# Reciprocal roots of eight and twelve columns: Newton steps on VectorE in place of powers on GpSimd

## The chip, the cores and the metric

The kernel runs on one core of one Trainium2 chip. The metric is the device time of one execution in microseconds, the median of several runs. TensorE (PE), VectorE (DVE), ScalarE (ACT), GpSimd (POOL) and SyncE (SP, which here only issues DMAs) run side by side and wait for each other by semaphores.

## What is computed

A two-layer backbone for 512 latent and 256 context tokens of width 1024. The first layer joins a gated DeltaNet (its inputs go through a convolution of five taps) with multi-head latent attention, the second a neighbourhood attention with grouped-query attention; a SwiGLU network follows each. The parts that the change touches are norms over the 64 channels of a head:

```python
def rms_norm(x, g):                       # queries and keys of grouped-query attention, layer two
    xf = x.astype(jnp.float32)
    y = xf * lax.rsqrt(jnp.mean(xf * xf, -1, keepdims=True) + NORM_EPS)
    return (y * g.astype(jnp.float32)).astype(x.dtype)

def l2_normalize(x):                      # queries and keys of the DeltaNet, layer one
    xf = x.astype(jnp.float32)
    return (xf * lax.rsqrt(jnp.sum(xf * xf, -1, keepdims=True) + NORM_EPS)).astype(x.dtype)
...
    qkv = jax.nn.silu(short_conv(qkv, conv_w))
    q, k, v = jnp.split(qkv, [GDN_QK_W, 2 * GDN_QK_W], axis=-1)
    q = l2_normalize(q.reshape(b, t_len, GDN_HEADS, GDN_DK)) * (GDN_DK ** -0.5)
    k = l2_normalize(k.reshape(b, t_len, GDN_HEADS, GDN_DK))
```

## The kernel before

Tokens are tiled by 128. Matmuls run in three products of a high and a low half (`mm3`, L198 to L200; in `tok_proj` L548 to L550), so every weight is split on arrival: `split` copies the high half on ScalarE (L181) and subtracts on VectorE (L182). The order of the instructions on each engine is not the order of the program: `TileContext(nc, schedule_with_timeline_sim=True)` plans it, from the order of the program as priority and from its own estimate of what each instruction takes; a few `issue_after` blocks and manual dependencies pin single places.

Convolution stage, layer one. A loop takes twelve blocks of 128 channels, in the order 4 to 7, 0 to 3, 8 to 11. For each, `chan_proj` multiplies the block out on TensorE (tile `qkv`), and the first half of `conv_tail` copies it (L702, L703), convolves it with five VectorE instructions (tile `cy`, L705 and L707) and puts a silu over it (tile `cz`, L709). The second half of `conv_tail` belongs to the block before: TensorE transposes it back into two PSUM banks `pa` and `pb` (L714), ScalarE squares it (L723), VectorE sums the squares over 64 channels to twelve columns, six tiles of tokens by two heads (L726), `rsqrt_` makes the reciprocal root, and VectorE multiplies the two banks by it (L730). Blocks 0 to 7, queries and keys, take this way, so there are eight calls; blocks 8 to 11 are only copied. The product goes to DRAM and, for the keys (4 to 7), through four more GpSimd products (`ek`, `kd`, L741). GpSimd also makes the tiles `gi` (L674) in the first part of the stage, and scales the small projection of the latent attention (L768, L769). The banks `pa` and `pb` come from the tag `v`, which has two banks; the transposes of `mla_latent` (tile `smT`, L775) take a bank of the same tag. The gate projection (`gate_evac`, L842 to L844) runs in the middle of the loop.

Head norms, layer two. `head_norm` runs for four tiles of latent queries (eight columns), `keys_norm` for the keys (eight and four columns). Each squares on ScalarE (L1897, L1920), sums on VectorE (L1900, L1923), takes the root, multiplies on VectorE (L1902, L1925), multiplies by the gain on GpSimd (L1903, L1926) and rotates, on VectorE and GpSimd (`rope`, L394 to L399). Squares and the rotation's products share one buffer, tag `hsq`. In the same stretch the modulation of the second layer is summed on VectorE: `Mod.step` loads a row block (`mraw`) through SP into one of two buffers and adds it with L255. All loads of weights go through the same SP queue, in order.

`rsqrt_` is two GpSimd instructions: an add (L222) and a power with a tile of -0.5 (L229). It has seven call sites; three of them are changed: L728, L1901 and L1924. The others (norms of one or two columns, and L1305 in `gdn_out`, eight columns) stay.

Of the kernel before, what the change touches and what calls it, by code (L numbers as in the profile page):

```python
# [150 lines left out]
F32 = mybir.dt.float32  # L151
F32R = mybir.dt.float32r
F16 = mybir.dt.float16
I32 = mybir.dt.int32
AF = mybir.ActivationFunctionType
ALU = mybir.AluOpType
AX = mybir.AxisListType
PSUM = bass.MemoryType.PSUM
EPS = 1e-6
# [4 lines left out]
def emit(tc, A):  # L164
    nc = tc.nc
    V, S, G, T = nc.vector, nc.scalar, nc.gpsimd, nc.tensor
    es = ExitStack()

    def pool(name, stack, bufs=1, **kw):
        return stack.enter_context(tc.tile_pool(name=name, bufs=bufs, reuse_waits="tile", **kw))  # L170
# [4 lines left out]
    def bc(ap, n):  # L175

        return ap.unsqueeze(len(ap.shape)).to_broadcast(list(ap.shape) + [n])
# [26 lines left out]
    sm = pool("sm", es, bufs=4)  # L204
# [15 lines left out]
    def rsqrt_(out, ss, add):  # L220

        G.tensor_scalar(out, ss, add, None, ALU.add)  # L222
        n = 1
        for s in out.shape[1:]:
            n *= s
        nh = nhalf[:, :n]
        if len(out.shape) == 3:
            nh = nh.rearrange("p (a b) -> p a b", a=out.shape[1])
        G.tensor_tensor(out, out, nh, ALU.pow)  # L229


    cs = cp.tile([128, 8, 2], F32, name="cs", tag="cs")
# [466 lines left out]
    def conv_tail(i, pl, pc):  # L699
# [4 lines left out]
        y = cvp.tile([128, 772], F32, tag="cy", name="cy", bufs=2)  # L704
# [12 lines left out]
        if i >= 8:  # L717
            for ps, a, b in views:
                S.activation(dst[:, a:b, :], ps[:, :(b - a) * 128].rearrange("p (t c) -> p t c", c=128), AF.Copy)
        else:  # L720
            sq = cvp.tile([128, 12, 64], F32, tag="sq", name="sq")
            for ps, a, b in views:
                S.activation(sq[:, 2 * a:2 * b, :], ps[:, :(b - a) * 128].rearrange("p (t c) -> p t c", c=64), AF.Square,  # L723
                             scale=8.0 if i < 4 else 1.0)
            ss = sm.tile([128, 12], F32, tag="ss12", name="ss12")
            V.tensor_reduce(ss, sq, AX.X, ALU.add)  # L726
            r = sm.tile([128, 12], F32, tag="r12", name="r12")
            rsqrt_(r, ss, (64.0 if i < 4 else 1.0) * EPS)  # L728
            for ps, a, b in views:
                V.tensor_tensor(dst[:, a:b, :].rearrange("p t (h c) -> p t h c", h=2),  # L730
                                ps[:, :(b - a) * 128].rearrange("p (t h c) -> p t h c", h=2, c=64),
                                bc(r[:, 2 * a:2 * b].rearrange("p (t h) -> p t h", h=2), 64), ALU.mult)
# [312 lines left out]
    def r3(ap):  # L1045
        return ap.rearrange("p (h c) -> p h c", c=64)
# [846 lines left out]
    def head_norm(dst, ps, nh, gain, t, scale):  # L1893

        sq = bx.tile([128, 512], F32, tag="hsq", name="hsq")
        S.activation(dst, ps, AF.Copy)
        S.activation(sq[:, :nh * 64], dst, AF.Square, scale=scale)  # L1897
        ss = sm.tile([128, 8], F32, tag="oss", name="oss")
        r = sm.tile([128, 8], F32, tag="orr", name="orr")
        V.tensor_reduce(ss[:, :nh], r3(sq[:, :nh * 64]), AX.X, ALU.add)  # L1900
        rsqrt_(r[:, :nh], ss[:, :nh], scale * scale * 64.0 * EPS)  # L1901
        V.tensor_tensor(r3(dst), r3(dst), bc(r[:, :nh], 64), ALU.mult)  # L1902
        G.tensor_tensor(r3(dst), r3(dst), gain.unsqueeze(1).to_broadcast([128, nh, 64]), ALU.mult)  # L1903
        if t < 4:
            rope(bx.tile([128, 512], F32, tag="hsq", name="rp"), r3(dst), ropeg[:, t, 0:32], ropeg[:, t, 32:64], 32, nh)
# [9 lines left out]
    def keys_norm(a, b):  # L1915

        n = 2 * (b - a)
        x = gkt[:, a:b, :].rearrange("p t c -> p (t c)")
        sq = bx.tile([128, 512], F32, tag="hsq", name="hsq")
        S.activation(sq[:, :n * 64], x, AF.Square, scale=0.125)  # L1920
        ss = sm.tile([128, 8], F32, tag="oss", name="oss")
        r = sm.tile([128, 8], F32, tag="orr", name="orr")
        V.tensor_reduce(ss[:, :n], r3(sq[:, :n * 64]), AX.X, ALU.add)  # L1923
        rsqrt_(r[:, :n], ss[:, :n], EPS)  # L1924
        V.tensor_tensor(r3(x), r3(x), bc(r[:, :n], 64), ALU.mult)  # L1925
        G.tensor_tensor(r3(x), r3(x), gkn.unsqueeze(1).to_broadcast([128, n, 64]), ALU.mult)  # L1926
        if a:
            return
        x1, x2 = [gkt[:, 0:4, :].rearrange("p t (h c) -> p t h c", h=2)[:, :, :, i:i + 32] for i in (0, 32)]
        cb, sb = [ropeg[:, 0:4, i:i + 32].unsqueeze(2).to_broadcast([128, 4, 2, 32]) for i in (0, 32)]  # L1930
        tmp = bx.tile([128, 512], F32, tag="hsq", name="rp")
        ta, tb = [tmp[:, i:i + 256].rearrange("p (t h c) -> p t h c", t=4, h=2) for i in (0, 256)]
        V.tensor_tensor(ta, x2, sb, ALU.mult)
        V.tensor_tensor(tb, x1, sb, ALU.mult)
        G.tensor_tensor(x1, x1, cb, ALU.mult)
        G.tensor_tensor(x2, x2, cb, ALU.mult)
        G.tensor_tensor(x1, x1, ta, ALU.subtract)
        G.tensor_tensor(x2, x2, tb, ALU.add)
# [394 lines left out]
```

## Time and profile before

| | |
|---|---|
| time, median of 3 runs | 1955.46 us (1953.3 to 1959.17) |
| the profiled execution's own time | 1962.06 us |
| its span, on which all times of the trace are counted | 1960.3 us |
| mean granted TensorE clock of the span | 0.964 |
| busy: PE, DVE, ACT, POOL | 1825.0, 1411.3, 986.4, 765.9 us |

A row of a group gives line, engine, operation, what it writes and reads, and the count. "Idle before" is how long the engine stood still just ahead of these instructions, and what released it. [...] The names of tiles leave out numbers, so the roots of twelve and of two columns are both `r`.

### The profile page before, as it was taken

The numbers are of one execution on the slowest core, as the hardware profiler recorded it, in microseconds if no ns is written. First come the engines' busy times: TensorE is split into PE (matmuls) and PEld (weight loads), VectorE is DVE, ScalarE is ACT, GpSimd is POOL, SyncE is SP. The second block draws the span as 40 slices with busy tenths as digits, with TensorE's granted clock in tenths as the row PEclk, the third lists the DMA queues.
The fourth block names the chain that finished last, engine by engine and source line by source line (L and its number), as shares of the span: only waits on it lengthen the run. The fifth ranks groups of instructions, "written<-read, shape, count | busy, mean of one in ns | idle before, by whom it ended". The sixth has DMA issues, their size and how long they took to land.

```text
span 1960.3 us, 33838 instructions
## 1 busy us (share of the span) xinstructions
PE 1825.0 (93%) x12780; PEld 1504.9 (77%) x12780; DVE 1411.3 (72%) x2166; ACT 986.4 (50%) x1880; POOL 765.9 (39%) x702
## 2 busy tenths in 40 slices
PE   6989978988998989999999999989999979999998
PEld 4877854655665879999998777877655669999886
DVE  3687767677875596666567897886566589999654
ACT  4433466766874473333334346723355465455443
POOL 2287455354515246566561011253356123333002
PEclk8999988998998999999999999999999979999999
DMA  8255595556643633222227553685443213233221
GB/s 308 88 147 148 187 291 167 178 184 171 211 113 117 232 108 104 96 65 74 78 65 262 162 177 106 215 287 192 153 118 113 87 65 106 91 109 95 88 96 65
DMA packets 125751, 280.20 MB, mean 143 GB/s; under 512 B 12882, under 2 KB 43498, under 8 KB 125588
## 3 DMA queue, kind: packets, MB, share of 16 engines
q1 hardware_dynamic: 125588, 278.03, 44.9%
q8 instruction: 101, 1.65, 0.4%
q14 instruction: 62, 0.51, 0.1%
HBM read 226.15 MB, written 46.07 MB: 139 GB/s over the span
## 4 chain that ended last, share of the span: by engine, by line
PE 62%; DMA 5%; ACT 5%; DVE 4%; issue 2%; POOL 2%; SPq 0%; POOLq 0%; DVEq 0%; ACTq 0%
PE st L199 10%; PE st L200 10%; PE st L198 10%; PE dn L1719 5%; PE dn L1720 5%; PE dn L1721 5%; PE po L189 2%; DMA mraw<-in_wmb_dram 2%; PE y L1435 1%; PE y L1436 1%; PE y L1437 1%; PE st L1981 1%; PE st L1982 1%; PE naqk L198 1%; PE nav L548 1%
## 5 line engine op out<-in xcount | busy, mean ns | idle before, releaser
L198 PE MATMUL st<-ub,hi_gu 128*128 128x384 f32 (+1 forms) x1232 | 385.5, 314 | 8.4 <-ACT ub L181 8.4
L199 PE MATMUL st<-ub,hi_gu 128*128 128x384 f32 (+1 forms) x1232 | 384.3, 312 | 3.0 <-DVE ub L182 3.0
L200 PE MATMUL st<-ub,lo_gu 128*128 128x384 f32 (+1 forms) x1232 | 385.6, 313 | 0.0
L198 PEld LDWEIGHTS st<-ub,hi_gu 128*128 128x128 f32 x1232 | 234.2, 190 | 8.8 <-ACT ub L181 8.8
L199 PEld LDWEIGHTS st<-ub,hi_gu 128*128 128x128 f32 x1232 | 234.8, 191 | 3.7 <-DVE ub L182 3.6
L200 PEld LDWEIGHTS st<-ub,lo_gu 128*128 128x128 f32 x1232 | 233.4, 189 | 0.5
L181 ACT ACTIVATE hi_gu<-s 128x512 fp32r<-128x512 f32 x176 | 110.9, 631 | 173.6 <-PE st L199 161.0
L1719 PE MATMUL dn<-hi_wd,gh 128*128 128x512 f32 x440 | 174.5, 397 | 2.2 <-ACT gh L181 2.2
L1720 PE MATMUL dn<-lo_wd,gh 128*128 128x512 f32 x440 | 174.0, 396 | 0.0
L1721 PE MATMUL dn<-hi_wd,gl 128*128 128x512 f32 x440 | 162.7, 400 | 1.6 <-DVE gl L182 1.6
L182 DVE TENSOR_TENSOR lo_gu<-s,hi_gu 128x512 fp32r<-128x512 f32 x154 | 129.1, 839 | 44.3 <-ACT hi_gu L181 44.2
L182 DVE TENSOR_TENSOR lo_gu<-raw_gu,hi_gu 128x512 fp32r<-128x512 f32 x132 | 130.0, 998 | 41.2 <-ACT hi_gu L181 41.1
L181 ACT ACTIVATE hi_gu<-raw_gu 128x512 fp32r<-128x512 f32 x132 | 81.9, 629 | 98.5 <-PE st L199 92.8
L255 DVE SCALAR_TENSOR_TENSOR macc<-mraw,cs,macc 128x1024 f32<-128x1024 f32 x80 | 104.5, 1322 | 17.9 <-DMA mraw<-in_wmb_dram 13.9
L1629 POOL TENSOR_TENSOR s<-raw_gu 128x512 f32<-128x512 f32 x44 | 75.4, 1713 | 99.8 <-issue 62.6
L929 ACT ACTIVATE P<-st 128x512 f32<-128x512 f32 x128 | 73.0, 596 | 73.4 <-PE st L200 36.0
L1719 PEld LDWEIGHTS dn<-hi_wd,gh 128*128 128x128 f32 x440 | 82.7, 188 | 23.3 <-ACT gh L181 2.7
L181 ACT ACTIVATE gh<-g 128x512 fp32r<-128x512 f32 x76 | 47.7, 631 | 104.7 <-PE dn L1720 95.2
L1721 PEld LDWEIGHTS dn<-hi_wd,gl 128*128 128x128 f32 x440 | 82.0, 188 | 23.5 <-DVE gl L182 3.5
L182 DVE TENSOR_TENSOR gl<-g,gh 128x512 fp32r<-128x512 f32 x76 | 54.3, 719 | 61.8 <-ACT gh L181 56.3
L1720 PEld LDWEIGHTS dn<-lo_wd,gh 128*128 128x128 f32 x440 | 82.7, 188 | 20.4 <-issue 0.7
L1685 POOL TENSOR_TENSOR g<-g,up 128x512 f32<-128x512 f32 x38 | 55.7, 1466 | 89.0 <-DVE up L1634 57.5
(540 smaller groups left out, 4702.3 us busy)
## 6 DMA issues: line engine op xcount, KB each, us to landing
mraw<-in_wmb_dram SPq DMA_DIRECT2D x56, 512.0 KB
raw_wd<-in_wd_dram SPq DMA_DIRECT2D x55, 512.0 KB
raw_gu<-in_wg_dram SPq DMA_DIRECT2D x44, 512.0 KB
raw_gu<-in_wu_dram SPq DMA_DIRECT2D x44, 512.0 KB
cu<-in_wmb_dram SPq DMA_DIRECT2D x24, 512.0 KB
raw_m<-in_wmb_dram SPq DMA_DIRECT2D x16, 512.0 KB
raw_qkv<-in_wqkv_dram SPq DMA_DIRECT2D x12, 512.0 KB
raw_tok<-qk_d SPq DMA_DIRECT2D x12, 512.0 KB
```

The lines of the kernel that those rows point to most:

```text
L181: r = S.activation(hi, src, AF.Copy)
L182: (lo_eng or V).tensor_tensor(lo, src, hi.bitcast(F32), ALU.subtract)
L198: T.matmul(out, wh, xh, start=start, stop=False)
L199: T.matmul(out, wh, xl, start=False, stop=False)
L200: T.matmul(out, wl, xh, start=False, stop=stop)
L255: V.scalar_tensor_tensor(a, raw, cs[:, self.k, v:v + 1], a, ALU.mult, ALU.add)
L929: S.activation(P[:, :n], ps[:, :n], AF.Exp)
L1629: G.tensor_tensor(s3, a11, a21, ALU.subtract)
L1685: G.tensor_tensor(g, g, u, ALU.mult)
L1719: T.matmul(ps, gh[:, tsl], wh, start=start, stop=False)
L1720: T.matmul(ps, gh[:, tsl], wl, start=False, stop=False)
L1721: T.matmul(ps, gl_[:, tsl], wh, start=False, stop=stop)
```

## The change

A new helper `newton` computes the reciprocal root on VectorE: add the epsilon, take a first guess by arithmetic on the bits of the number (the exponent halved and negated), scale the number by -0.5, and run three Newton rounds of three instructions each; twelve instructions a call. It takes two scratch tiles from the pool `sm` (two buffers each). The calls in `conv_tail`, `head_norm` and `keys_norm` use it in place of `rsqrt_`: eight, four and two calls.

```diff
--- before.py
+++ after.py
@@ -227,6 +227,20 @@
         if len(out.shape) == 3:
             nh = nh.rearrange("p (a b) -> p a b", a=out.shape[1])
         G.tensor_tensor(out, out, nh, ALU.pow)
+
+    def newton(y, ss, add, t):
+
+        x, w = t
+        V.tensor_scalar(x, ss, add, None, ALU.add)
+        V.tensor_scalar(y.bitcast(I32), x.bitcast(I32), -0.5, float(0x5f3759df), ALU.mult, ALU.add)
+        V.tensor_scalar(x, x, -0.5, None, ALU.mult)
+        for _ in range(3):
+            V.tensor_tensor(w, y, y, ALU.mult)
+            V.tensor_tensor(w, w, x, ALU.mult)
+            V.scalar_tensor_tensor(y, w, 1.5, y, ALU.add, ALU.mult)
+
+    def newton_tiles(n):
+        return [sm.tile([128, n], F32, tag=f"nw{i}_{n}", name="nw", bufs=2) for i in range(2)]
 
 
     cs = cp.tile([128, 8, 2], F32, name="cs", tag="cs")
@@ -725,7 +739,7 @@
             ss = sm.tile([128, 12], F32, tag="ss12", name="ss12")
             V.tensor_reduce(ss, sq, AX.X, ALU.add)
             r = sm.tile([128, 12], F32, tag="r12", name="r12")
-            rsqrt_(r, ss, (64.0 if i < 4 else 1.0) * EPS)
+            newton(r, ss, (64.0 if i < 4 else 1.0) * EPS, newton_tiles(12))
             for ps, a, b in views:
                 V.tensor_tensor(dst[:, a:b, :].rearrange("p t (h c) -> p t h c", h=2),
                                 ps[:, :(b - a) * 128].rearrange("p (t h c) -> p t h c", h=2, c=64),
@@ -1898,7 +1912,7 @@
         ss = sm.tile([128, 8], F32, tag="oss", name="oss")
         r = sm.tile([128, 8], F32, tag="orr", name="orr")
         V.tensor_reduce(ss[:, :nh], r3(sq[:, :nh * 64]), AX.X, ALU.add)
-        rsqrt_(r[:, :nh], ss[:, :nh], scale * scale * 64.0 * EPS)
+        newton(r[:, :nh], ss[:, :nh], scale * scale * 64.0 * EPS, [x[:, :nh] for x in newton_tiles(12)])
         V.tensor_tensor(r3(dst), r3(dst), bc(r[:, :nh], 64), ALU.mult)
         G.tensor_tensor(r3(dst), r3(dst), gain.unsqueeze(1).to_broadcast([128, nh, 64]), ALU.mult)
         if t < 4:
@@ -1921,7 +1935,7 @@
         ss = sm.tile([128, 8], F32, tag="oss", name="oss")
         r = sm.tile([128, 8], F32, tag="orr", name="orr")
         V.tensor_reduce(ss[:, :n], r3(sq[:, :n * 64]), AX.X, ALU.add)
-        rsqrt_(r[:, :n], ss[:, :n], EPS)
+        newton(r[:, :n], ss[:, :n], EPS, [x[:, :n] for x in newton_tiles(12)])
         V.tensor_tensor(r3(x), r3(x), bc(r[:, :n], 64), ALU.mult)
         G.tensor_tensor(r3(x), r3(x), gkn.unsqueeze(1).to_broadcast([128, n, 64]), ALU.mult)
         if a:
```

## Rows read from the trace of the kernel before

**Rows 1.** The page, part 1: busy us (share of the span) xinstructions of each engine

```profile
PE 1825.0 (93%) x12780; PEld 1504.9 (77%) x12780; DVE 1411.3 (72%) x2166; ACT 986.4 (50%) x1880; POOL 765.9 (39%) x702
```

**Rows 2.** Stretches: us, busy (x) of PE, PEld, DVE, ACT, POOL; PEclk, DMA share, GB/s

```profile
100.00:150.00 50.00, 42.83 (x239) 36.84 (x238) 40.48 (x44) 16.76 (x40) 40.91 (x29) 0.93 0.55 153
150.00:200.00 50.00, 48.52 (x231) 39.18 (x229) 35.44 (x42) 15.81 (x40) 35.99 (x26) 1.00 0.54 152
```

**Rows 3.** Groups by line, 60 to 245 us: busy us, mean ns | idle before, releaser

```profile
L229 POOL TENSOR_TENSOR r<-r,nhalf 128x12 f32<-128x12 f32 x8 | 20.8, 2603 | 0.6
...
L730 DVE TENSOR_TENSOR tk<-pa,r 128x512 f32<-128x512 f32 x8 | 5.5, 691 | 18.5 <-POOL r L229 18.5
```

**Rows 4.** Waits of PE, 100 to 245 us: total us, times, longest us

```profile
PE smT L775 <- DVE tk L730: 7.5, 4, 3.9
```

**Rows 5.** DVE in order of time: start us, us, what [idle before <-releaser]

```profile
109.93 0.95 DVE L726 TENSOR_REDUCE ss<-sq 128x12 f32<-128x768 f32 x1
...
125.20 0.69 DVE L730 TENSOR_TENSOR tk<-pa,r 128x512 f32<-128x512 f32 x1 [4.20 <-POOL r L229]
...
145.61 0.69 DVE L730 TENSOR_TENSOR tk<-pa,r 128x512 f32<-128x512 f32 x1 [2.19 <-POOL r L229]
...
164.82 0.69 DVE L730 TENSOR_TENSOR tk<-pa,r 128x512 f32<-128x512 f32 x1 [3.14 <-POOL r L229]
```

**Rows 6.** POOL in order of time, 110 to 197 us

```profile
110.57 2.76 POOL L674 TENSOR_TENSOR gi<-g_c,glx 128x512 f32<-128x512 f32 x2
...
120.14 2.76 POOL L674 TENSOR_TENSOR gi<-g_c,glx 128x512 f32<-128x512 f32 x2
122.87 2.30 POOL L229 TENSOR_TENSOR r<-r,nhalf 128x12 f32<-128x12 f32 x1
...
195.30 1.34 POOL L843 TENSOR_TENSOR gt<-gt,c_onorm 128x512 f32<-128x512 f32 x1
```

**Rows 7.** PE in order of time, around 126 and 146 us

```profile
126.03 0.87 PE L775 MATMUL smT<-ident,sml 128*128 128x128 f32 x3 [3.92 <-DVE tk L730]
...
146.45 0.52 PE L775 MATMUL smT<-ident,sml 128*128 128x128 f32 x3 [2.07 <-DVE tk L730]
```

**Rows 8.** Stretches of one and three us around the two waits of rows 7

```profile
125.00:126.00 1.00, 0.00 (x0) 0.00 (x0) 0.80 (x2) 0.00 (x0) 0.17 (x1) 0.50 0.93 244
...
130.00:131.00 1.00, 1.00 (x4) 0.81 (x3) 0.96 (x2) 0.00 (x0) 0.04 (x1) 0.50 0.97 353
...
145.00:148.00 3.00, 1.55 (x14) 1.57 (x15) 2.35 (x4) 0.45 (x1) 1.86 (x2) 1.00 0.12 39
```

**Rows 9.** DVE in order of time, 50 to 100 us: small operations

```profile
69.75 0.17 DVE L394 TENSOR_TENSOR rp<-sml,ropem 128x16 f32<-128x16 f32 x1
69.84 0.17 DVE L395 TENSOR_TENSOR rp<-sml,ropem 128x16 f32<-128x16 f32 x1
...
80.28 2.02 DVE L624 SCALAR_TENSOR_TENSOR t<-t,t 128x96 f32<-128x96 f32 x7
```

**Rows 10.** Two lines of DVE, ns min/median/max; then POOL and DVE in order of time

```profile
L2147 DVE TENSOR_TENSOR mxa<-mxa,mxb x8: 153/159/525, 1376.3 to 1496.6; 128x4 f32<-128x4 f32 x8
...
L1986 DVE CAST mxr<-mxa x16: 161/310/1093, 1376.5 to 1516.1; 128x4 fp32r<-128x4 f32 x16
...
461.83 1.27 POOL L973 TENSOR_TENSOR acc<-acc,P 128x512 f32<-128x512 f32 x1
...
462.58 0.55 DVE L951 TENSOR_TENSOR mxr<-mxa,mxb 128x4 fp32r<-128x4 f32 x1
```

**Rows 11.** 1260 to 1350 us: a POOL group; ACT in order of time; waits of PE

```profile
L229 POOL TENSOR_TENSOR orr<-orr,nhalf 128x8 f32<-128x8 f32 x5 | 10.3, 2056 | 0.4
...
1298.49 0.63 ACT L1897 ACTIVATE hsq<-gqt 128x512 f32<-128x512 f32 x1 [9.78 <-POOL gqt L398]
...
PE nav L548 <- ACT gvt L1909: 3.0, 1, 3.0
PE gkv L548 <- DVE xl L1946: 2.6, 1, 2.6
```

## The prediction

> **What bounds the kernel now.** I read the page's first part, then busy time by stretch, then the two stretches that hold the fourteen calls that change: eight in the convolution stage (`conv_tail`, 100 to 245 us) and six in the head norms of the second layer (1260 to 1350 us). TensorE is busy 93% of the span [rows 1], so a saving counts only where TensorE stands still or runs slow. In the convolution stage it is idle 7.2 us between 100 and 150 us and 1.5 us in the next 50; VectorE is busy 40.5 and 35.4 us of these fifties, GpSimd 40.9 and 36.0 [rows 2]. Next come the groups by line: the power on twelve columns takes GpSimd 2.6 us, eight times, and the multiply behind it (L730) made VectorE stand still 18.5 us in all for the root [rows 3]. Then TensorE's own waits: the transposes of L775 waited 7.5 us in four waits on that L730 [rows 4], since they take the PSUM bank that L730 reads.
>
> So the path is: reduce, root, L730, bank free, TensorE. In the first call the reduce starts at 109.93 and L730 only at 125.20 [rows 5]: GpSimd's power starts at 122.87, behind other products [rows 6]. TensorE waited 3.92 us there and 2.07 us at the second call [rows 7]. [...]
>
> **The change, part by part.** *Removed:* two GpSimd instructions a call: the add, and the power of 2.6 us at twelve columns [rows 3] or 2.06 at eight [rows 11]. GpSimd is not the bound; what counts is the delay between reduce and multiply, and the queue on GpSimd that the root leaves.
>
> *Added:* three VectorE instructions and three rounds of three, twelve a call, 168 in all. The trace has no twelve-column Newton step. The nearest row of a two-input operation is one on four columns, 0.153 us at best [rows 10]. For a step that depends on the one before it, a chain of seven at 96 columns took 2.02 us, each lasting 0.258 us: 0.26 plus six steps of 0.293, so some 0.035 us lie between one's end and the next's start. Where nothing depends, two small operations start 0.09 us apart [rows 9]. So a call costs VectorE 12 x 0.09 = 1.1 us where the steps fall between other work, and 12 x (0.155 + 0.035) = 2.3 us where they follow each other. I take the upper end for the first call and 1.7 us, the middle, where a few products stand between.
>
> The eight calls may thus spend 18.5 / 96 = 0.193 us a step before VectorE loses more than it gains from the wait that goes; the chained estimate is 0.19. VectorE as a sum wins nothing by this; any gain must come from L730 no longer standing behind GpSimd's queue. The order on each engine is planned anew by the scheduler of the framework, so the steps need not stand right behind the reduce. Queued behind them on VectorE are the next channel block's convolution (L705, L707), the weight splits of L182, and in the second layer the modulation sums of L255 and the copies L1946. The weights and the modulation rows are loaded through SP's one queue, and a late L182 or L255 holds up the next load there; SP gets no new instruction.
>
> *First call.* TensorE asked at 126.03 - 3.92 = 122.1 us. Earliest: reduce end 110.9 plus 2.3 is 113.2, no wait and no low clock. That gives back 3.9 us, and half of the 5.5 us or so from 126.03 on at half clock, 2.7: -6.6 us. Latest: VectorE's work ahead of L730 ends at 125.20 - 4.20 = 121.0; 2.3 for the steps, and if each of the eight GpSimd products of that stretch (the first two at 110.57, the last two at 120.14 [rows 6]) holds up one step by the worst that a small operation shows, 1.09 less its own 0.16 us, 7.4 more: L730 at 130.7, +5.5 us. I take 121.0 + 2.3 = 123.3, the present order with the steps put in, since that row already contains convolution steps slowed beside GpSimd: 1.9 us of the wait goes, and a wait of 2.0 is like the one after which the clock stayed at 1.00, so the 2.7 us go too: -4.6 us.
>
> *Second and third calls.* VectorE is free at 145.61 - 2.19 = 143.42 and at 164.82 - 3.14 = 161.68 [rows 5]. With 1.7 us the second L730 comes at 145.1, -0.5 us. For the third I add one collision of 0.9 us: 164.3, -0.5 us. Ends: both waits gone, 2.07 + 1.5 (what rows 4 and 7 leave for the other two), -3.6; or 2.3 us of steps and three collisions in the third, +3.0. *The other five:* TensorE hardly waits there: 0, with +2.3 as the end for a call without VectorE idle.
>
> *Head norms.* One scratch tile ties the four tiles of tokens together: the next square on ScalarE waits for GpSimd's rotation of the last (9.78 us in one wait), and TensorE waits 3.0 us for copies queued behind it [rows 11]. The root shrinks from 2.06 us plus the add to at most 2.3; three calls lie ahead of that wait, and I count 0.3 us each, some -1.0 us. Ends: the 3.0 us gone; or 2.3 us more ahead of each of the two waits of [rows 11], whose other one (2.6 us) is on L1946 on VectorE: +4.6.
>
> *Sum:* -4.6 - 0.5 - 0.5 - 1.0 = -6.6 us on the profiled execution's 1962.06 us (span 1960.3 and 1.8 around it). The median of the runs, 1955.46, is 0.34% below that; scaled, 1955.46 x (1 - 6.6 / 1962.06) = 1948.9, said as 1949.
>
> **The rivals.** *Everything that waits on L730 goes.* The first call comes at its early end, the three smaller waits go, and the second layer gains 2: -6.6 - 3.6 - 2 = -12.2, 1943 us. For it: the reduce is 15 us ahead of L730. Against it: VectorE has other work in between, and the planner mixes it in.
>
> *The wait moves.* TensorE finds another late operand, since VectorE is about as full as before: 0, 1955.5 us. For it: in the second fifty microseconds TensorE is already 97% busy [rows 2], and a sum of 0.193 against 0.19 us leaves VectorE no slack. A variant of the same size is that the plan comes out otherwise and hands back in one place what it wins in another.
>
> *GpSimd holds up the steps: slower.* A small operation beside a GpSimd product waits for it to end: at 462.58 one on four columns took 0.55 us, to 463.13, where GpSimd's product ran from 461.83 to 463.10 [rows 10]. Medians of 0.16 and 0.31 us stand against worst cases of 0.53 and 1.09. In GpSimd's order of time 16 products lie between reduce and multiply in the first five calls, the first at 110.57, the last at 195.30 [rows 6], eight of them in the first call; at 0.9 us each that is 14 us on VectorE, beside 8 x 2.3 = 18 us of steps, for 18.5 saved. What gets through to TensorE is the late end of the first call, 5.5, and of the next two, 3.0: about +8.5, 1964 us. It decides from the point where a step costs more than 0.193 us on average. Against it: in calls two and four GpSimd runs dry soon after the reduce, and in the second layer it idles there.
>
> [...]
>
> **How the numbers follow.** The measurement can tell about 0.3%, 5.9 us, from no change. Chances: forecast 0.40 (spread about 4 us either way), everything goes 0.17, the wait moves 0.23, held up by GpSimd 0.20. Faster by over 0.3% (below 1949.6): a little over half of the forecast's and all of the second, 0.40. Within: the rest of the forecast's, most of the third, and a little of the last, 0.39. Slower: 0.21. Range: down to 1939, 10 us below the forecast (the ends of all terms together would be -15.5 and +15.4, which I don't expect at once), and up to 1964, the slow rival's price; what lies outside is half of that rival and little below.
>
> **What would show it.** Right: no idle of VectorE before L730, small operations near 0.16 us, and TensorE's wait on L730 at the first call under 2.5 us with the clock at 1.00 from 120 to 135 us. The slow rival: steps of 0.5 us and more while GpSimd runs products. The moved wait: L730 early, but TensorE idle as long on something else. The prediction is wrong if the plan puts L730 behind a whole convolution, or if stages that the change doesn't touch shift by more than the sum.

## The result and the profile after

| | before | changed |
|---|---|---|
| time, median of 4 runs on one chip | 1956.94 us (1953.3 to 1959.17) | 1989.95 us (1988.47 to 1994.26) |
| ratio | 1 | 1.0169, 95% interval 1.0153 to 1.0185 |
| span of the profiled execution | 1960.3 us | 1986.7 us |

The change makes the kernel slower by 33 us in the medians and by 26.4 us between the two profiled executions. The forecast was 1949 us, range 1939 to 1964.

The page's first part, changed kernel (columns as in [rows 1]):

```profile
PE 1820.0 (92%) x12780; PEld 1503.2 (76%) x12780; DVE 1432.1 (72%) x2334; ACT 986.7 (50%) x1880; POOL 721.3 (36%) x674
```

VectorE has 168 instructions and 21 us more, GpSimd 45 us less. TensorE does the same work in a longer span, so it waits more somewhere. Busy time by stretch tells where. First the kernel before, then the changed one (columns as in [rows 2]; PEclk is the share of its full clock that TensorE was granted):

```profile
100.00:240.00 140.00, 128.76 (x689) 108.42 (x688) 106.88 (x132) 51.19 (x122) 93.67 (x65) 0.98 0.55 164
240.00:300.00 60.00, 43.37 (x305) 32.41 (x303) 37.74 (x57) 34.38 (x69) 32.66 (x27) 0.82 0.92 285
1280.00:1400.00 120.00, 110.41 (x600) 92.35 (x598) 81.85 (x114) 37.47 (x77) 44.03 (x42) 0.96 0.64 212
```

```profile
100.00:240.00 140.00, 133.97 (x719) 113.85 (x718) 108.95 (x200) 54.42 (x125) 65.37 (x51) 0.98 0.56 167
240.00:300.00 60.00, 34.23 (x198) 25.54 (x197) 33.34 (x62) 22.75 (x47) 19.33 (x18) 0.74 0.49 168
1280.00:1400.00 120.00, 102.34 (x526) 86.93 (x525) 93.83 (x182) 35.69 (x79) 33.61 (x28) 0.91 0.68 222
```

Up to 240 us TensorE is ahead by 5.2 us of work, near the 5.6 us that the prediction gave the first three calls. Between 240 and 300 us it loses 9.1 us of work and finds its clock at 0.74 instead of 0.82. Between 1280 and 1400 us it does 8.1 us less (the changed kernel comes to the same work some 18 us later, so these two rows don't hold the same work).

What TensorE waits for between 100 and 310 us in the changed kernel (us in all, times, longest; compare [rows 4]; the lines are those of before plus 14), and VectorE's group of the multiply with its idle time (compare [rows 3]):

```profile
PE pa L728 <- DVE tk L744: 7.7, 1, 7.7
PE kup L198 <- DVE qkl L182: 7.0, 1, 7.0
...
PE smT L789 <- DVE tk L744: 1.9, 1, 1.9
```

```profile
L744 DVE TENSOR_TENSOR tk<-pa,r 128x512 f32<-128x512 f32 x8 | 5.5, 690 | 0.5
```

VectorE no longer stands still for the root: 0.5 us instead of 18.5. TensorE's four waits for the multiply, 7.5 us, have become one of 1.9 us at the first call and one of 7.7 us after the eighth. Another 7.0 us go to a split (`qkl`) that VectorE makes behind the seventh call's steps; the part on the memsets comes back to it. So VectorE's idle time went, and the multiply still comes later, from the second call on. Reduce to multiply, call by call, from VectorE's rows in order of time (start of `ss` to start of `tk<-pa`, us):

| call | 1 | 2 | 3 | 4 | 5 | 6 | 7 | 8 | sum |
|---|---|---|---|---|---|---|---|---|---|
| before | 15.3 | 6.6 | 9.1 | 6.5 | 7.7 | 5.1 | 5.1 | 4.5 | 59.8 |
| changed | 14.0 | 8.9 | 8.3 | 9.3 | 10.9 | 14.5 | 16.5 | 7.1 | 89.6 |

The delay adds up from call to call: the multiply comes 0.6 us early in the first call and 2.4, 2.3, 7.5, 12.8, 14.0, 23.4 and 26.7 us late in the next seven. Of the last figure 24.0 us are there when the eighth reduce starts. Between reduce and multiply VectorE starts 72 other instructions in the eight calls, where it started 35 before.

The eighth call shows how. Before, VectorE in order of time, then GpSimd:

```profile
236.57 0.95 DVE L726 TENSOR_REDUCE ss<-sq 128x12 f32<-128x768 f32 x1
...
238.02 1.02 DVE L707 SCALAR_TENSOR_TENSOR cy<-xpad,c_conv,cy 128x772 f32<-128x772 f32 x1
...
240.09 1.02 DVE L707 SCALAR_TENSOR_TENSOR cy<-xpad,c_conv,cy 128x772 f32<-128x772 f32 x1
241.02 0.69 DVE L730 TENSOR_TENSOR tk<-pa,r 128x512 f32<-128x512 f32 x1
```

```profile
237.93 2.30 POOL L229 TENSOR_TENSOR r<-r,nhalf 128x12 f32<-128x12 f32 x1
```

Changed:

```profile
260.56 0.95 DVE L740 TENSOR_REDUCE ss<-sq 128x12 f32<-128x768 f32 x1 [3.49 <-ACT sq L737]
261.43 0.61 DVE L719 TENSOR_SCALAR cy<-xpad,c_conv 128x772 f32<-128x772 f32 x1
261.95 0.17 DVE L234 TENSOR_SCALAR nw<-ss 128x12 f32<-128x12 f32 x1
262.07 1.02 DVE L721 SCALAR_TENSOR_TENSOR cy<-xpad,c_conv,cy 128x772 f32<-128x772 f32 x1
263.01 0.17 DVE L235 TENSOR_SCALAR r<-nw 128x12 int32<-128x12 int32 x1
263.13 1.02 DVE L721 SCALAR_TENSOR_TENSOR cy<-xpad,c_conv,cy 128x772 f32<-128x772 f32 x1
...
266.22 0.16 DVE L240 SCALAR_TENSOR_TENSOR r<-nw,r 128x12 f32<-128x12 f32 x1
266.42 0.17 DVE L238 TENSOR_TENSOR nw<-r 128x12 f32<-128x12 f32 x1
...
267.70 0.69 DVE L744 TENSOR_TENSOR tk<-pa,r 128x512 f32<-128x512 f32 x1
```

Before, the power ran on GpSimd while VectorE convolved the next block. Now VectorE does both: between the first of the steps the plan lets five instructions of the convolution in (0.6 to 1.0 us), and the steps behind each wait for it.

GpSimd has a part in this too. Six of the 96 steps of the eight calls took 1.00 to 6.27 us, the others 0.25 at most, and each of the six ends with a GpSimd instruction. Together they are 10.8 us longer than usual: 6.1 in the seventh call beside memsets (see there), 4.7 in the first, fourth and fifth beside two-input products. One of these, VectorE and GpSimd:

```profile
187.80 1.23 DVE L239 TENSOR_TENSOR nw<-nw 128x12 f32<-128x12 f32 x1
```

```profile
187.71 1.30 POOL L857 TENSOR_TENSOR gt<-gt,c_onorm 128x512 f32<-128x512 f32 x1 [5.97 <-ACT gt L856]
```

What the eighth multiply releases, in the changed kernel: the bank for the next block's transposes, the store of the keys and queries, their load, and the DeltaNet's first transposes. TensorE's rows and SP's:

```profile
268.54 1.09 PE L728 MATMUL pa<-ident,cz 128*128 128x128 f32 x4 [7.72 <-DVE tk L744]
...
277.18 1.06 PE L1075 MATMUL kTp<-ident,raw_tok 128*128 128x128 f32 x4
```

```profile
268.75 0.37 SPq L748 DMA_DIRECT2D qk_d<-tk  x1
...
273.19 0.33 SPq L1150 DMA_DIRECT2D raw_tok<-qk_d  x1
```

Before, the same line (L1061 there):

```profile
249.70 0.63 PE L1061 MATMUL kTp<-ident,raw_tok 128*128 128x128 f32 x4
```

So the DeltaNet starts 27.5 us late. Some of it is won back: the first matmul of the output projection (`y`) comes at 645.0 instead of 626.6, 18.4 us late, and that distance stays until the second layer (first `gkv` matmul 1287.8 and 1306.0). There the six roots grow from 23.6 us in all to 53.2. The first one, 4.9 us before and 14.8 now, VectorE, changed:

```profile
1288.71 0.67 DVE L1914 TENSOR_REDUCE oss<-hsq 128x8 f32<-128x512 f32 x1
1289.70 1.28 DVE L269 SCALAR_TENSOR_TENSOR macc<-mraw,cs,macc 128x1024 f32<-128x1024 f32 x1 [0.32 <-DMA mraw<-in_wmb_dram]
1290.90 0.17 DVE L234 TENSOR_SCALAR nw<-oss 128x8 f32<-128x8 f32 x1
...
1298.41 0.17 DVE L238 TENSOR_TENSOR nw<-orr 128x8 f32<-128x8 f32 x1
1301.10 1.28 DVE L269 SCALAR_TENSOR_TENSOR macc<-mraw,cs,macc 128x1024 f32<-128x1024 f32 x1 [2.53 <-DMA mraw<-in_wmb_dram]
1302.31 0.16 DVE L239 TENSOR_TENSOR nw<-nw 128x8 f32<-128x8 f32 x1
...
1303.52 0.69 DVE L1916 TENSOR_TENSOR gqt<-gqt,orr 128x512 f32<-128x512 f32 x1
```

Here the steps stand behind modulation sums that themselves wait for their DMA, 0.32 and 2.53 us in the two shown. The end is 26.4 us late (18.2 from the first layer, 8 from this one).

### The profile page after: what moved, and what is told of

It reads as the page before. It is cut to its first block, busy times and chain, and to the rows that moved or that the text cites. A ratio compares the mean times of both kernels' runs of the same rounds, so it can differ in the third digit from the quotient of the medians.

```text
span 1986.7 us, 33971 instructions
## 1 busy us (share of the span) xinstructions
PE 1820.0 (92%) x12780; PEld 1503.2 (76%) x12780; DVE 1432.1 (72%) x2334; ACT 986.7 (50%) x1880; POOL 721.3 (36%) x674
## 5 line engine op out<-in xcount | busy, mean ns | idle before, releaser
L269 DVE SCALAR_TENSOR_TENSOR macc<-mraw,cs,macc 128x1024 f32<-128x1024 f32 x80 | 105.0, 1327 | 18.6 <-DMA mraw<-in_wmb_dram 14.5
L182 DVE TENSOR_TENSOR gl<-g,gh 128x512 fp32r<-128x512 f32 x76 | 54.0, 716 | 61.7 <-ACT gh L181 56.2
```

The lines of the kernel that those rows point to most:

```text
L182: (lo_eng or V).tensor_tensor(lo, src, hi.bitcast(F32), ALU.subtract)
L269: V.scalar_tensor_tensor(a, raw, cs[:, self.k, v:v + 1], a, ALU.mult, ALU.add)
```

## The experiments

Theories. **1:** the root's time counts, and it grew because twelve dependent steps share VectorE with other work. **2:** GpSimd holds up the steps (the prediction's slow rival). **3:** VectorE has no room for 168 more instructions. **4:** the plan came out worse by chance. Ratios are against the kernel before beside it on the same chip, with 95% intervals; the medians of before there were 1960.1 to 1961.6 us. "Roots" is the sum of the eight reduce-to-multiply times, "start" the first matmul of the DeltaNet (before: 59.8 and 249.7 us). These two come from one execution of each kernel, as all times of a trace do, and late in the trace they can differ by some 6 us between executions: the kernel before and the run with the head norms alone have the same instructions in the first layer, and come to the second layer's first `gkv` matmul 6.1 us apart.

### Which calls, and whether it is the steps or the waiting for them

**Convolution stage alone.**

```diff
-newton(r[:, :nh], ...)   # and in keys_norm
+rsqrt_(r[:, :nh], ...)
```

> Newton's steps in the eight calls of the convolution stage alone, the power in the six head norms. Theory 1 (latency: the twelve dependent steps are planned between other VectorE work, so that the time from reduce to multiply grows, and the eighth call of the convolution stage starts the DeltaNet): the first layer ends 18 us late as in the changed kernel (first gkv matmul 1288.0 to 1306.2) and the second layer adds nothing, so 1956 + 18 = 1974 us, 1971 to 1978. Theory 2 (GpSimd holds up the steps where both run): the stage has GpSimd's collisions too, so also some 15 to 20 us; it is told apart by the trace (steps of 0.5 us and more). Theory 3 (VectorE has no room for 168 more instructions): 96 of 168, evenly spread, 33 x 96 / 168 = 19 us. Theory 4 (the plan came out worse elsewhere): no relation, -5 to +30.

Measured: 1980.52 us, 1.0100 (1.0077 to 1.0123), +19.6 us. Roots 87.7, start 275.6. The first layer carries about what the trace of the changed kernel put on it. The time is 2.5 us above theory 1's range and meets theory 3's 19 and theory 2's 15 to 20 us as well, so this run doesn't choose between them.

**Head norms alone.**

```diff
-newton(r, ss, ..., newton_tiles(12))   # conv_tail
+rsqrt_(r, ss, ...)
```

> Newton's steps in the six head norms of layer two alone. Theory 1: the first layer is that of the kernel before to the instruction; the loss is what the changed kernel lost after 1350 us, 26.4 - 18.2 = 8 us at the end, up to 15 us if the loss at the maxima (33.7 - 18.2) is not won back: 1964 to 1972 us. Theory 2: no collisions there to speak of, since GpSimd loses the power: 0 to 3 us, 1956 to 1960. Theory 3: 72 of 168 steps, 14 us.

Measured: 1967.4 us, 1.0031 (1.0015 to 1.0047), +6 us. Between theory 1's lower end and theory 2's upper one; theory 3's 14 us is out. The profiled execution shows the loss behind the first layer: it reaches the first `gkv` matmul 6.1 us ahead of before and ends 0.8 us behind it. None of the 72 steps took over 0.17 us there, so no part of this loss is GpSimd's holding them up.

**Steps that nobody waits for.**

```diff
-newton(r, ss, ...)
+newton(unused, ss, ...)   # twelve steps into a tile that is never read
+rsqrt_(r, ss, ...)        # the root that is used: the power, on GpSimd
```

> All fourteen calls take the root by the power on GpSimd as before, and VectorE makes the 168 Newton steps beside it into a tile that nobody reads. Theory 1: nobody waits for the steps, so the time from reduce to multiply stays near that of before (59.7 us in eight calls): 1953 to 1962 us. Theory 2: the steps still stand beside GpSimd's products and are held up, and the work behind them with them: +15 us or more. Theory 3: VectorE has all the added work and none of the removed waits: 1985 us or more.

Measured: 1956.9 us, 0.9981 (0.9968 to 0.9995). Roots 52.9, start 251.2. The page's first part:

```profile
PE 1811.6 (93%) x12780; PEld 1492.9 (77%) x12780; DVE 1452.4 (74%) x2334; ACT 986.3 (51%) x1880; POOL 767.5 (39%) x702
```

VectorE does as many instructions as in the changed kernel and is busy 41 us longer than before, 20 longer than there, beside all of GpSimd's work, and the kernel is no slower, even 0.2% faster. Theory 3 falls. So does theory 2 for the whole: single steps took up to 1.48 us here (0.17 in the median), and it cost nothing while nobody waited for them. It keeps the share counted above, 10.8 us of the 30 by which the eight roots grew.

**A later root without VectorE.**

```diff
 G.tensor_tensor(out, out, nh, ALU.pow)
+if slow:   # the same fourteen calls
+    G.tensor_tensor(out, out, ones[:, :n], ALU.pow)
```

> The kernel before with a second power (to the one) behind the first in the same fourteen calls, on GpSimd: the root comes some 2.6 us later in each, the result is the same, and VectorE has nothing added. Theory 1 (what counts is how late the root comes): the eight calls lose up to 21 us against 30 in the changed kernel, so +8 to +22 us: 1969 to 1983. Theory 2 and 3 (VectorE's steps or its sum): VectorE is as before, +0 to +4.

Measured: 1979.78 us, 1.0094 (1.0074 to 1.0114), +18 us. Roots 87.6, start 265.3. The eighth call, GpSimd and then VectorE:

```profile
250.90 0.54 POOL L222 TENSOR_SCALAR r<-ss 128x12 f32<-128x12 f32 x1 [1.68 <-DVE ss L728]
251.52 3.03 POOL L229 TENSOR_TENSOR r<-r,nhalf 128x12 f32<-128x12 f32 x1
254.63 2.27 POOL L231 TENSOR_TENSOR r<-r,ones 128x12 f32<-128x12 f32 x1
```

```profile
256.93 0.69 DVE L732 TENSOR_TENSOR tk<-pa,r 128x512 f32<-128x512 f32 x1
```

With nothing added to VectorE the sum of the roots is nearly the changed kernel's (87.6 and 89.6), and more than half of the loss appears. That speaks for theory 1. It isn't the delay alone, though: GpSimd has a longer queue here, whatever stands behind the second power is later too, and this run doesn't separate the two.

**First three calls, last five.**

```diff
-newton(r, ss, ...)
+if i in (4, 5, 6):          # the other run: (7, 0, 1, 2, 3)
+    newton(r, ss, ...)
+else:
+    rsqrt_(r, ss, ...)      # head norms: rsqrt_ in both
```

> Newton's steps in the first three calls of the convolution stage alone, the power in the other five and in the head norms. The prediction's terms for these calls sum to -5.6 us: 1955. Theory 1: here VectorE gets no fewer other instructions between the steps (eight, eight and seven), the multiply comes at 124.6, 148 and 167 us as in the changed kernel against 125.2, 145.6 and 164.8; the stage is not full yet, so -2 to +4: 1959 to 1965. If it takes +15 or more, the loss isn't in the later calls.

Measured: 1966.01 us, 1.0024 (1.0007 to 1.0041), +4.7 us. Roots 61.7, the eighth multiply at 247.4, start 258.7. The prediction's -5.6 us for these calls doesn't come, and theory 1's upper end of +4 is just passed; TensorE is early (last `qkv` matmul at 241.4 instead of 244.5) and the eighth multiply late.

> Newton's steps in calls four to eight of the convolution stage alone, the power in the first three and in the head norms: the other half of the run on the first three calls, which took +0.24%. The prediction's term for these five was 0, with +2.3 us as the end: 1956 to 1964 beside a kernel before at 1961.5. Theory 1 (late root, and the eighth call starts the DeltaNet): +12 to +20 us, 1973 to 1981, since in the changed kernel calls four to seven had 25 of the 30 us by which reduce to multiply grew.

Measured: 1970.31 us, 1.0049 (1.0031 to 1.0067), +9.6 us, above the prediction's 0 to 2.3 and under theory 1's 12 to 20. Roots 82.0, start 269.4. The two halves add to 14 us and the whole stage took 19.6, so the calls don't add up singly. The later ones seem to lose more than the first three, but the intervals (6.1 to 13.1 and 1.4 to 8.0 us) overlap.

A late start is not the loss itself. Three runs have twelve steps a call in this stage alone: starts 9.0, 19.7 and 25.9 us late go with 4.7, 9.6 and 19.6 us. What wins the rest back, and why not always the same share, no run here shows.

### How many steps

**One round, and none.**

```diff
-for _ in range(3):
+for _ in range(1):   # the other run: range(0)
```

> The changed kernel with one round of Newton's steps instead of three, so six dependent steps a call instead of twelve (the root is good to a few parts in a thousand only). Theory 1 (each dependent step lets other VectorE work of 0.6 to 1 us in ahead of the next one): half the steps, half the growth of reduce to multiply, 59.8 + 15 = 75 us in the eight calls instead of 89.6; the time halfway, 1961 + 16 = 1977 us, 1970 to 1982. Theory 3 (VectorE's sum) the same half. Theory 4 (the plan came out worse once, whatever the steps): no order by the number of steps.

Measured: 1955.77 us, 0.9960 (0.9941 to 0.9979). Roots 43.1, start 243.1. Faster than before, against the 1970 to 1982 us that theory 1 gave: half the steps are not half the loss, since with six of them the roots take less time than with the power.

> The changed kernel with the guess alone, three dependent steps a call and no round (the root is off by up to some per cent). Theory 1: a quarter of the steps, reduce to multiply 59.8 us or less in the eight calls, since the power and its queue go too; 1950 to 1966 us, and at the lower end the price of the forecast's wait that goes. Theory 4: no order by the number of steps.

Measured: 1946.73 us, 0.9925 (0.9910 to 0.9940), 3 us under theory 1's range. Roots 32.0, start 244.8; here the last `qkv` matmul (239.8) and not the root is near it. Without the rounds the result of the kernel has a relative error of 0.18, so this run only prices the steps.

**A shorter chain of good accuracy.** With w = x y^2 the root is y times a polynomial in w; its leading factor goes into the scale of x, so each degree is one instruction.

```diff
-V.tensor_scalar(x, ss, add, None, ALU.add)
+V.tensor_scalar(x, ss, 10.24, add * 10.24, ALU.mult, ALU.add)
-V.tensor_scalar(y.bitcast(I32), x.bitcast(I32), -0.5, float(0x5f3759df), ALU.mult, ALU.add)
-V.tensor_scalar(x, x, -0.5, None, ALU.mult)
-for _ in range(3): ...
+V.tensor_scalar(y.bitcast(I32), x.bitcast(I32), -0.5, float(-550020641), ALU.mult, ALU.add)
+V.tensor_tensor(w, y, y, ALU.mult)
+V.tensor_tensor(w, w, x, ALU.mult)
+V.scalar_tensor_tensor(x, w, -4.2, w, ALU.add, ALU.mult)
+V.scalar_tensor_tensor(x, x, 7.0, w, ALU.add, ALU.mult)
+V.scalar_tensor_tensor(y, x, -7.0, y, ALU.add, ALU.mult)
```

This has seven steps; a degree less makes six (good to 1e-4), a degree more eight.

> The changed kernel with a shorter chain of the same accuracy as two of Newton's rounds (6 parts in a million): one instruction that adds and scales, the guess, and five instructions for a polynomial of the third degree, seven dependent steps a call instead of twelve. Theory 1: between the run with six steps (0.4% under the kernel before) and the changed kernel, by the number of steps 1961 + 33 x (7 - 8) / 4 = about 1953 us, taking 8 steps as the point where it breaks even on the line through the runs with 6 and 12 steps (7.2); 1950 to 1963. Theory 4 (chance of the plan): anything up to 1990.

> As the run with seven steps, with a polynomial of the fourth degree: eight dependent steps a call and an accuracy near that of the changed kernel (8 parts in ten million). Theory 1: on the line through 6 steps (-0.4%) and 12 steps (+1.69%) eight steps stand at +0.3%, 1967 us; 1958 to 1972. Theory 4: no order by the number of steps.

> As the run with seven steps, with a polynomial of the second degree: six dependent steps a call, good to one part in ten thousand (the run with one round: some two parts in a thousand). Theory 1: the time goes by the number of steps, so as the run with one round, 0.996: 1953 us, 1949 to 1959, beside a kernel before at 1961. By chance of the plan alone: up to +0.5%.

> Six dependent steps in the eight calls of the convolution stage alone, the power in the six head norms. Theory 1: the convolution stage's gain is what the run with one round showed at 630 us (first y matmul 617.5 against 626.6, 9 us early); the head norms by the power keep it: 1952 us, 1948 to 1958. If the head norms made the gain, 1960.

| dependent steps a call | ratio | 95% interval | roots, us | start, us |
|---|---|---|---|---|
| 3 (no round) | 0.9925 | 0.9910 to 0.9940 | 32.0 | 244.8 |
| 6 (one round) | 0.9960 | 0.9941 to 0.9979 | 43.1 | 243.1 |
| 6 (polynomial) | 0.9995 | 0.9982 to 1.0008 | 53.8 | 254.0 |
| 6 (polynomial, convolution stage alone) | 0.9984 | 0.9972 to 0.9996 | 54.0 | 254.1 |
| 7 (polynomial) | 1.0004 | 0.9984 to 1.0025 | 61.6 | 254.9 |
| 8 (polynomial) | 1.0051 | 1.0033 to 1.0068 | 71.1 | 258.7 |
| 12 (the change) | 1.0169 | 1.0153 to 1.0185 | 89.6 | 277.2 |
| 12 (the change, again) | 1.0143 | 1.0114 to 1.0172 | 88.8 | 273.4 |

Measured medians of the polynomials: 1961.02 us (seven), 1972.09 (eight), 1959.41 (six) and 1957.14 (six, with the power left in the head norms). Seven came within theory 1's range but 8 us above the 1953 that it gave, eight and six just past the upper edge of theirs, six in the convolution stage alone just inside, so theory 1's line lies too low for the polynomials.

The time goes with the steps, and the change breaks even at six or seven of them. Two kernels with six steps everywhere differ by 0.35%: in the seventh call of the slower one sixteen other instructions stand between reduce and multiply, eight in the other, and it takes 11.8 us against 6.8. So theory 4 can have a share of that size. Of these kernels three are faster than before with an interval clear of 1: the one without a round, the one with one round, whose root is good to 0.2% only, and by 3 us the polynomial in the convolution stage alone.

### The order, and the memsets

**Steps right behind the reduce.** The order of the loop is turned round, and the next block's convolution is queued behind the multiply, so that in four of the eight calls nothing stands between the steps.

```diff
 tail = conv_tail(i, pl, pc)
-next(tail)
 if prev:
     next(prev, None)
+with tc.issue_after(muls[-1]) if 0 < n < 9 else ExitStack():
+    next(tail)
```

> The changed kernel with one order turned round: the second half of a block's tail is traced ahead of the first half of the next block's, and that next block's convolution is queued on VectorE behind the multiply, so that in the first seven calls at most two other instructions stand between the reduce and the multiply instead of six to nineteen; the eighth keeps eight. Theory 1: reduce to multiply 3 to 5 us in calls one to seven, the stage's loss goes: 1989.95 - 18 = 1972 us, 1963 to 1975, the loss of the head norms staying. Theory 2 and 3: the same steps beside the same GpSimd work and the same VectorE sum: 1985 to 1990 us. Against all: the convolution, which before filled the wait for the root, now stands behind it, and that could cost up to 5 us a call.

> The kernel before with the order that the run with the steps first had: the next block's convolution queued on VectorE behind the multiply, the root by the power. VectorE then stands still during the power. If the order alone costs, by taking away the work that VectorE does beside the root, this is slower than before by 25 us or more (the root is 3.9 us a call against 2.5 for the steps, seven calls, beside the 30 us of that run). If it is at +0 to +10, the earlier run lost by its steps.

Measured: with the steps 1992.06 us, 1.0159 (1.0137 to 1.0182); with the power 1988.29 us, 1.0136 (1.0113 to 1.0160). The roots fell to 42.3 and 42.7 us, the start came at 269.6 and 279.4. A call with the steps, VectorE:

```profile
181.66 0.95 DVE L742 TENSOR_REDUCE ss<-sq 128x12 f32<-128x768 f32 x1 [1.23 <-ACT sq L739]
182.65 0.17 DVE L234 TENSOR_SCALAR nw<-ss 128x12 f32<-128x12 f32 x1
...
184.77 0.17 DVE L240 SCALAR_TENSOR_TENSOR r<-nw,r 128x12 f32<-128x12 f32 x1
185.15 0.69 DVE L746 TENSOR_TENSOR tk<-pa,r 128x512 f32<-128x512 f32 x1 [0.20 <-DVE r L240]
```

TensorE's largest wait there (100 to 290 us), with the steps and then with the power:

```profile
PE pa L730 <- ACT cz L725: 25.6, 4, 8.7
```

```profile
PE pa L716 <- ACT cz L711: 30.6, 6, 7.5
```

In calls three to six the root follows the reduce at once (3.49 us from reduce to multiply in the call shown), and now the transposes wait for the silu of a convolution that starts late. TensorE's last `qkv` matmul comes at 264.6 and 274.4 instead of 244.5, and the start follows it, no longer the eighth multiply (242.8 and 247.7). Theory 1 gave 1972 for the steps, and the time lies above the 1985 to 1990 of theories 2 and 3 too; theory 1 had left out that the convolution lies on the same loop. Reduce, root, multiply, transposes and the next convolution follow each other, and before the change root and convolution were the two parts of it that ran side by side. With the power the order alone costs 27 us, as much, so this loss isn't the steps', and the pair says nothing for or against theory 1.

**The memsets.** In the seventh call of the changed kernel the guess took 6.27 us. VectorE, and GpSimd beside it:

```profile
243.55 6.27 DVE L235 TENSOR_SCALAR r<-nw 128x12 int32<-128x12 int32 x1
244.50 5.32 DVE L721 SCALAR_TENSOR_TENSOR cy<-xpad,c_conv,cy 128x772 f32<-128x772 f32 x1
```

```profile
243.26 1.30 POOL L1160 TENSOR_TENSOR R<-g_c,gv 128x512 f32<-128x512 f32 x1
244.50 5.29 POOL L1156 MEMSET cu<- 128x2048 f32 x3
```

Behind these steps stands the split `qkl` for which TensorE waited 7.0 us.

```diff
-G.memset(raws[slot], 0.0)
+V.memset(raws[slot], 0.0)
```

> The changed kernel with the DeltaNet's zeroing of its buffers (GpSimd's memsets of 128x2048, three of which took 5.29 us in a row from 244.5 us, while the guess of the seventh call took 6.27 us on VectorE) made on VectorE instead. If those memsets held up the seventh call and through it the DeltaNet, the guess takes about 0.2 us again and 3 to 6 us come back: 1984 to 1987 beside 1990. If theory 1's mixed steps carry nearly all, -2 to +4, since VectorE gets the memsets to do.

> The changed kernel once more, unaltered, on the same chip as the three below: 1.015 to 1.0185 of the kernel before, so 1985 to 1997 us.

> The kernel before with the zeroing of the DeltaNet's buffers on VectorE instead of GpSimd, all roots by the power. If the zeroing is late only behind Newton's steps: -3 to +4 us, since here the eighth multiply is over at 242 us before the first memset at 244.7. If it holds up VectorE in the start of the DeltaNet whatever the root does: -7 to -14 us, as in the changed kernel.

> Seven dependent steps and the zeroing on VectorE. Seven steps alone stood at 1.0004. If the zeroing is worth the same there as in the changed kernel, -7 to -14 us: 1947 to 1955 beside 1961. If it is worth only what lies on the chain of a late seventh call, -1 to -4.

| memsets on | changed | before | seven steps |
|---|---|---|---|
| GpSimd | 1.0169, again 1.0143 | 1 | 1.0004 |
| VectorE | 1.0098 (1.0073 to 1.0123) | 1.0046 (1.0031 to 1.0061) | 1.0030 (1.0014 to 1.0047) |

Measured: 1980.35, 1988.75 (the repeat, its ratio just under the 1.015 expected), 1970.84 and 1965.65 us. With the memsets moved no guess takes over 0.18 us, TensorE's 7.0 us wait for `qkl` is gone, and 9 to 14 us of the loss go, more than the 3 to 6 expected (roots 84.5, start 269.0). In the other two kernels the same move costs 5 to 9 us, which was expected of neither. So the meeting of the seventh root with the memsets is a part of the loss, a third or so, and the rest is there without it. How much exactly stays open, since the move has a price of its own: if that is 5 to 9 us here too, the meeting is worth more. Why the move costs anything in the other two is not shown. This wait is GpSimd's larger share in the longer roots; the products that the prediction had in mind held up five steps beside it.

## Why the prediction was wrong

*What bounds the kernel* and *first call*: these held, in the main. The first L730 (now L744) was forecast at 123.3 and came at 124.63, its wait at TensorE fell from 3.92 to 1.92 us. The clock term came in half: after 1.92 us of waiting the rows from 126 to 129 us stand at 0.50 to 0.53, the next at 0.77, and from 130 on at 1.00, where before, after 3.92 us of waiting, six rows from 125 to 131 us stood at 0.50 [rows 8]. So a wait of this length isn't always like the 2.07 us one, around which the clock stayed at 1.00.

*Second and third calls*: TensorE's waits went, as forecast, but not for the reason given. The multiplies, forecast at 145.1 and 164.3, came at 148.06 and 167.13, 2.4 and 2.3 us later than before instead of 0.5 earlier. The terms of the three calls summed to -5.6 us; TensorE had done 5.2 us more work by 240 us, and its last `qkv` matmul came 6.2 us early. That lead didn't reach the end: it ended in TensorE's waits of 7.0 and 7.7 us behind the seventh and eighth call, and in the run with these three calls alone the kernel lost 4.7 us.

*The price of a step* held as well: 0.193 us from start to start on average in an undisturbed chain ((184.77 - 182.65) / 11), against the estimate of 0.19, and 2.3 us for twelve. The agreement is a little lucky: ten of the eleven distances are 0.20 to 0.21 us, and one, between two steps of which neither uses the other's result, is 0.08.

*"The other five: TensorE hardly waits there: 0, with +2.3 as the end"*: this step failed. These five alone took +9.6 us, with the first three +19.6, and the eighth multiply came 26.7 us late. Two things were wrong in the step. It asked only who waits for the multiply today. TensorE did not, but the eighth multiply, at 241.02, also opens the DeltaNet through the store and load of `qk_d`; that release never stood in the prediction's list of what is queued behind. It had hardly any slack: the load was issued at 244.86, in the run with the second power, where TensorE waited for this load (3.8 us in two waits), its matmul came 4.0 us after the load's issue, as it did in the changed kernel (273.19 and 277.18); and in the kernel before TensorE was busy with other work until 249.63. That makes some 0.8 us (an estimate from these rows) before a later multiply is a later start. And it took VectorE's time for the steps (1.1 us where they fall between other work) for the root's time. Where they fall between other work, each step waits for what was let in: the last five roots grew by 29 us (28.9 to 58.3), not by 11.5 at the most; 8.3 of the 29 are steps that GpSimd held up. "A call without VectorE idle" was taken as the harmless case; it is the one in which convolution and root add up.

*Head norms, -1.0 with ends at -3.0 and +4.6*: the same mistake. The six roots grew by 30 us; the run with these alone took +6 us (2.9 to 9.2), and in the profile of the changed kernel this stretch and what follows lost 8.

*The rivals.* *GpSimd holds up the steps* had the right sign at 1964 us and a part of the mechanism. Of its 16 collisions of 0.9 us, five came, 0.8 to 1.1 us each, beside the products for `gi` and `gt` (L688, L857); ten steps that ran wholly beside GpSimd's scaling of `sml` (L782, L783), which it had counted too, took 0.16 to 0.25 us. The sixth and longest, with the memsets, it didn't name. It was to get through to TensorE in the first three calls, and that isn't where the loss arose. *The wait moves* was right in kind: the waits of 7.0 and 7.7 us are TensorE finding another late operand. It was priced at 0 because the new wait was taken to be as long as the old ones. The rest is the prediction's last sentence, that the plan might put the multiply behind a whole convolution: it had no chance and no price there. It could have had both: the convolution of a block is one instruction of 0.6 us and four of 1.0, and with twelve steps of 0.19 that makes some 7 us a call where calls six and seven had 5.1 and the eighth 4.5. The eighth then took 7.1.

*0.193 us a step as break-even* was a sum over all eight calls, 18.5 us of VectorE's idle time over 96 steps. But it isn't spread evenly: calls seven and eight had 0.6 and 0 of it, and the eighth is the one on the path. The runs put the point at six or seven steps a call.

*The sums and the signs.* Two ends don't come out of their rows: the second and third calls with 2.3 us of steps and three collisions give about +2.0 us, not +3.0, and the lower ends of all terms -13.2, not -15.5. Neither moves the forecast; the slow rival's price would be 1 us lower. The signs of being right were nearly all met (0.5 us of VectorE idle before the multiply, most steps near 0.17 us, TensorE's first wait under 2.5 us; only the clock fell below 1.00 from 126 to 130 us), and the kernel still lost 33 us: they looked at the first call, and the loss arose behind it.

## What to carry to other kernels

An engine's idle time in front of a wait is no reserve if what it waits for runs on another engine beside its own work: moving that work over turns two things side by side into two in a row (here VectorE's idle time before the multiply fell from 18.5 to 0.5 us and the eight roots grew from 59.8 to 89.6), and only the time from the first input to the last use says what it costs. A chain of short dependent steps takes, under a scheduler that fills gaps, the time of everything that is let in between, so count its steps and shorten it (here six or seven were free, and each one from there to twelve cost some 0.3%, the meeting with the memsets included). Before setting a term to zero, follow the result past the engine that waits for it today to the next stage that starts with it.

## What the runs showed of the hardware

A small VectorE instruction on 128x12 waited for GpSimd's memsets: 6.27 us in both profiled executions of the changed kernel, in the one shown until the third memset's end at 249.8 us; in the run with the convolution stage alone 4.52 us, ending with the second of three; with the memsets on VectorE the same instruction took 0.17 us at most in the eight calls of that stage. So in these rows the wait lasted over two and three memsets in a row.

In the changed kernel the five steps that started while a two-input GpSimd product on 128x512 ran (`gi`, `gt`) took 1.00 to 1.27 us and ended with it; the ten that ran wholly beside GpSimd's scaling of `sml` took 0.16 to 0.25.

In the run with the steps first (182.65 to 185.15 us), an undisturbed step of 128x12 lasted 0.16 to 0.17 us, and the next started 0.20 to 0.21 us after its start, 0.08 where neither uses the other's result; from the last step's start to the multiply's it was 0.38 us there, and 0.20 to 0.28 in six calls of the changed kernel. Zeroing 128x2048 took 1.76 us on VectorE (the runs with the memsets there) and on GpSimd 1.81 in the kernel before and 2.13 in the changed one, 5.29 for three in a row in both.
